# Adaptive modulation as one evenly paced stream of tiles with two buffers of its own, in a two-block network on one Trainium2 core

## The chip, the cores and the metric

The kernel runs on one core of a Trainium2 chip, in float32. The metric is the device time of one execution in microseconds (us): the median of three runs is 2570.3 us (2568.92 to 2570.32).

The engines are TensorE (PE: matrix products, with PEld for the loading of the stationary operand), VectorE (DVE), ScalarE (ACT), GpSimd (POOL) and SyncE (SP), which here issues nearly all transfers. Each engine works through its own instructions in the order in which the program lists them.

## The reference

256 tokens of 1024 features pass a first block of two layers and a second block of two layers. A layer of the first block has three sections: a feed-forward section, a mixer (convolution, state-space and sparse-attention branches, merged by gates), and a second feed-forward section. Ahead of each section the rows are shifted and scaled, and behind it gated, by vectors that depend on a second input `c` alone:

```python
h = x
for l in range(DEPTH):                                   # DEPTH = 2
    mod = (jax.nn.silu(c) @ ada_w[l] + ada_b[l]).reshape(bsz, 3, 3, 1, D_MODEL)
    u = modulate(h, mod[:, 0, 0], mod[:, 0, 1])          # h * (1 + scale) + shift
    y = swiglu_ffn(u, ffn_w_gate[l, 0], ffn_w_up[l, 0], ffn_w_down[l, 0])
    h = layer_norm(DN_ALPHA * h + MACARON_WEIGHT * mod[:, 0, 2] * y, ln_g[l, 0], ln_b[l, 0])
    u = modulate(h, mod[:, 1, 0], mod[:, 1, 1])
    y = hybrid_token_mixer(u, ...)
    h = layer_norm(DN_ALPHA * h + mod[:, 1, 2] * y, ln_g[l, 1], ln_b[l, 1])
    u = modulate(h, mod[:, 2, 0], mod[:, 2, 1])
    y = swiglu_ffn(u, ffn_w_gate[l, 1], ffn_w_up[l, 1], ffn_w_down[l, 1])
    h = layer_norm(DN_ALPHA * h + MACARON_WEIGHT * mod[:, 2, 2] * y, ln_g[l, 2], ln_b[l, 2])
```

`ada_w[l]` has 1024 x 9216 elements: nine vectors of 1024 outputs per layer, 18 in all, here called modulation rows and named (l, j) with j from 0 to 8. Their weights are 75 MB of the 479 MB that the kernel reads. The second block has a mixer and a feed-forward section per layer and no modulation.

## The kernel before

**Weight units.** All weights come in units of 128 x 1024 float32 (512 KB). `load_half` (L177) takes a buffer `raw` from a ring of four (`wraw`, L111) and issues the load on SyncE (L181). `split_half` (L184) then writes the high part `hi` on ScalarE (L187) and the low part `lo` on VectorE (L188) to a second ring of four (`wsp`, L112). TensorE makes three products for each exact one (`hi`x`hi`, `hi`x`lo`, `lo`x`hi`): `gemm_w` (L284 to L286) with the weights stationary, 24 products of 256 columns a unit, or `gemm_x` (L297 to L299) with the activations stationary.

**Order.** The program is written out by hand as a list of items. `run` (L258) walks through it: for each unit it first splits units ahead until four are live (so three units ahead of the one in work), then issues the unit's products and what evacuates them, and last calls `step_sides` (L224). A side is a Python generator with a rate: at each unit it is advanced by that many steps, and each step issues its instructions at that place of every queue. Convolution, attention, state space, early splits of the next section, fetches for the next boundary, and the modulation are sides. `drain` and `force` (L1192) run a side ahead until it is done or a condition holds. `late_load` (L235) places a load behind the last weight load.

**Modulation.** A tile is one eighth of a modulation row: its 128 outputs stand on the partitions, the 1024 weights of each along the columns. `ada_tile` (L493) loads it with `load_half`, so through the same ring of four raw buffers and the same queue as the weights, and one VectorE instruction (L495) multiplies it by the broadcast silu(c) and adds it up into one column. `ada` (L497) is the side that does this for a list of rows, eight tiles a row; after each third row a step turns the row on TensorE (L513) and writes it to DRAM (L516), from where `Ln.fetch` (L572) broadcasts it as the gate of the boundary. silu(c) itself is made by `silu_c` (L479) in a buffer `stk` that the attention uses too; each section that runs tiles loads and transforms it again, by a broadcast load of 512 KB and an activation.

**Who does which rows.** Rows (0,0) and (0,1) are made ahead of the first products (`First.start`). The other 16 are given to sections of the first block by lists at the end (L1881 and after):

```python
nm = 2 if l == 0 else 0
ada0 = [(l, j) for j in range(2 if l == 0 else 3, 8 - nm)]
adam = [(l, j) for j in range(8 - nm, 8)] if nm else []
ada1 = [(l, 8)] + ([(l + 1, j) for j in range(3)] if l + 1 < DEPTH else [])
```

That is 32 tiles in the first feed-forward section, 16 in the first mixer (from its unit 80 on, at 0.75 a unit), 32 in the second feed-forward section, 40 in the third, none in the second mixer, 8 in the fourth feed-forward section. The feed-forward rates (`ffn_section`, L1845) are 0.8, 0.8, 1.0 and 0.6 a unit. `Ln.prefetch` (L563), called ahead of the last units of a section, drains what is left and computes the affine columns of the next section from its shift and scale rows (`mod_affine`, L519).

A later feed-forward section has 11 hidden chunks of four units and 22 units of the down projection, 66 in all; the first makes four of its chunks in `First.start` and has 50 left. A mixer of the first block has 117 units. The convolution's taps (L1187) are 480 VectorE instructions, a side too.

Of the kernel before, what the change touches and what calls it, by code (L numbers as in the profile page):

```python
# [31 lines left out]
# columns of the constant array  # L32
# [16 lines left out]
# columns of the per-layer parameter array of the first block  # L49
# [15 lines left out]
# columns of the per-layer parameter array of the second block  # L65
# [8 lines left out]
class Chunk:  # L74
    """A weight chunk in DRAM, [128, n]; each half loaded when it is split."""
# [19 lines left out]
class Unit:  # L95
    """Half a chunk (1024 columns per partition): split into exact parts, then multiplied by mm."""
# [9 lines left out]
def net_kernel(ctx, tc, a, out, dbg=None):  # L106
# [128 lines left out]
    def late_load(dst, src):  # L235
        # queued behind the weights asked for so far
# [8 lines left out]
    def own_bank(half, key, *ins):  # L245
        # the first half of an accumulator does not wait for the products of the second, in another bank
# [4 lines left out]
    def behind(ins):  # L251
        # what follows is issued after these instructions on their engines
# [26 lines left out]
    def gemm_w(ps, w, xT, wk=0, xk=0, nk=KT):  # L279
        # ps[128 features, 256 tokens]; weights stationary  # L280
# [10 lines left out]
    def gemm_x(ps, xT, k, tt, w, kk, cs, first, last):  # L291
        # ps[128 tokens, n]; activations stationary
# [8 lines left out]
    def tt_split(group, body, between, halves=1):  # L301
        # units held so that all products of token tile 0 come first, then `between`, then token tile 1
# [22 lines left out]
    def proj_cols(src, xT, evac, n=2):  # L325
        # n*128 columns, transposed: evac(ps[128, n*256])
# [10 lines left out]
    def proj_rows(srcs, xT, evac, c=512, between=None, psf=None):  # L337
        # c columns as rows of tokens: evac(tt, ps[128, c]) for both token tiles
# [25 lines left out]
    def row_accum(y, src, xTf, k0, first, last):  # L364
        # y[tt][128 tokens, 1024] += two k-tiles of a chunk
# [14 lines left out]
    def row_tail(y, parts, between, room):  # L380
        # the last k-tiles, token tile 0 first; parts: (chunk, half, operand, k, first)
# [12 lines left out]
    def rows_to_T(row, tt, xT, k0=0, nk=KT, gcol=None, bcol=None):  # L394
        # row [128 tokens, nk*128] -> split transposed operand, with an optional affine per feature
# [22 lines left out]
    def norm_T(norm, row, tt, xT, gcol, bcol=None):  # L418
        # norm(columns) fills part of row; two feature tiles at a time to the split transposed operand
# [38 lines left out]
    def rsqrt_col(dst, src, scale, eps):  # L458
        # dst = (src*scale + eps)^-0.5
# [11 lines left out]
    mods, pcols, adas = {}, {}, []  # L471
# [7 lines left out]
    def silu_c(first=False):  # L479
        crow = f(rt("stk", 8 * P, 1, F32R))  # L480
        if not first:
            late_load(crow, a["c"].to_broadcast([P, D]))
            S.activation(crow, crow, AF.Silu)
            return crow
# [6 lines left out]
        return crow  # L491
# [5 lines left out]
    def ada(items, after=(), crow=None):  # L497
        # silu(c) . w + b, the output features on the partitions
        if crow is None:
            crow = silu_c()  # L500
        for l, j in items:
# [16 lines left out]

    def mod_affine(l, i):  # L519
        # columns G, B with u = n*G + B for the normalised n  # L520
# [22 lines left out]
    def start_fetch(nx):  # L543
        # what the section boundary needs beside the weights, one load per unit
# [1615 lines left out]
```

## Time and profile before

| | before |
|---|---|
| median of 3 runs | 2570.3 us |
| span of the profiled execution, first to last instruction | 2563.5 us |
| TensorE busy | 2443.6 us (95%) |
| VectorE busy | 1847.3 us (72%) |
| ScalarE busy | 1349.5 us (53%) |
| read from memory | 478.79 MB, 189 GB/s over the span |
| modulation tiles in raw buffers | 128 of 512 KB, 156.2 us of VectorE |

The profile is of one execution; its own time outside the span is not given, and the median of the runs lies 6.8 us above the span. Busy time is what an engine spends in instructions; products overlap each other in TensorE's pipeline, so a busy TensorE can still run at less than its full pace, and the count of its instructions in a stretch tells the pace. An idle time ahead of an instruction is put down to the instruction or transfer that ended it. The sections are told apart by their last products, behind which the transposes of the next boundary (L432) follow.

### The profile page before, as it was taken

How to read it: one execution, taken by the hardware profiler on the slowest of the kernel's cores; microseconds unless marked ns; L12 is line 12 of the kernel's file. 1: busy time of each engine (PE TensorE's matmuls, PEld its weight loads, DVE VectorE, ACT ScalarE, POOL GpSimd, SP SyncE). 2: the span in 40 equal slices, each digit the busy share in tenths (PEclk: the TensorE clock that was granted, in tenths of full speed). 3: DMA queues.
4: the chain of work that ended last, by engine and by line, in shares of the span. 5: the costliest groups of instructions: out<-in, count | busy, mean ns of one | idle time of the engine just before them, and what ended most of it. 6: DMA issues, size and time to landing. Idle time of an engine off the chain costs nothing.

```text
span 2563.5 us, 42615 instructions
## 1 busy us (share of the span) xinstructions
PE 2443.6 (95%) x16604; PEld 2205.0 (86%) x16604; DVE 1847.3 (72%) x3270; ACT 1349.5 (53%) x2360; POOL 70.0 (3%) x128
## 2 busy tenths in 40 slices
PE   8988999998999899899999999999899999999999
PEld 6877889898888888788898999899789888789888
DVE  7667888899776677668988996755766545656554
ACT  5334666654553453345666546545465555555554
POOL 0000000000000000000000000000100000100000
PEclk9999999999999999999999999999999999999999
DMA  8886632246868868875522356567345466436464
GB/s 326 271 277 224 197 111 87 80 146 231 290 207 274 291 195 283 269 251 166 164 70 81 123 181 226 195 212 247 123 126 179 159 185 220 139 100 221 141 187 142
DMA packets 134795, 486.83 MB, mean 190 GB/s; under 512 B 15633, under 2 KB 16193, under 8 KB 134594
## 3 DMA queue, kind: packets, MB, share of 16 engines
q1 hardware_dynamic: 134018, 482.93, 57.4%
q8 instruction: 130, 2.13, 0.3%
q10 hardware_dynamic: 576, 1.19, 0.1%
q14 instruction: 71, 0.58, 0.1%
HBM read 478.79 MB, written 5.27 MB: 189 GB/s over the span
## 4 chain that ended last, share of the span: by engine, by line
PE 58%; DMA 17%; DVE 14%; ACT 7%; issue 3%; POOL 1%; ACTq 0%; DVEq 0%; POOLq 0%; SPq 0%
PE mm L284 9%; PE mm L285 9%; PE mm L286 9%; DVE lo L188 6%; PE y L297 6%; PE y L298 6%; PE y L299 6%; DMA raw<-in_wg_dram 4%; DMA raw<-in_adaw_dram 4%; ACT hi L187 4%; DMA raw<-in_wd_dram 3%; DMA raw<-in_wu_dram 3%; DVE ca L1187 3%; PE tp L972 2%; PE tp L963 1%
## 5 line engine op out<-in xcount | busy, mean ns | idle before, releaser
L187 ACT ACTIVATE hi<-raw 128x1024 fp32r<-128x1024 f32 (+1 forms) x676 | 714.2, 1059 | 796.4 <-PE mm L285 285.0
L188 DVE TENSOR_TENSOR lo<-raw,hi 128x1024 fp32r<-128x1024 f32 (+1 forms) x676 | 824.7, 1222 | 385.1 <-ACT hi L187 379.1
L286 PE MATMUL mm<-xTh,lo 128*128 128x256 f32 x2896 | 829.1, 286 | 20.6 <-DVE lo L188 20.5
L284 PE MATMUL mm<-xTh,hi 128*128 128x256 f32 x2896 | 831.9, 287 | 17.5 <-ACT hi L187 9.9
L285 PE MATMUL mm<-xTl,hi 128*128 128x256 f32 x2896 | 825.1, 285 | 1.4 <-DVE xTl L455 1.4
L286 PEld LDWEIGHTS mm<-xTh,lo 128*128 128x128 f32 x2896 | 553.9, 191 | 27.5 <-DVE lo L188 26.9
L284 PEld LDWEIGHTS mm<-xTh,hi 128*128 128x128 f32 x2896 | 554.1, 191 | 26.0 <-ACT hi L187 13.4
L285 PEld LDWEIGHTS mm<-xTl,hi 128*128 128x128 f32 x2896 | 553.6, 191 | 5.2 <-DVE xTl L455 2.2
L299 PE MATMUL y<-hi,q 128*128 128x512 f32 x664 | 263.0, 397 | 0.0
L298 PE MATMUL y<-lo,q 128*128 128x512 f32 x552 | 220.7, 400 | 11.5 <-DVE lo L188 11.4
L297 PE MATMUL y<-hi,q 128*128 128x512 f32 x552 | 220.2, 401 | 4.1 <-ACT hi L187 2.2
L1187 DVE SCALAR_TENSOR_TENSOR ca<-av,pcol,ca 128x244 f32<-128x244 f32 (+22 forms) x480 | 206.8, 460 | 0.5
L495 DVE SCALAR_TENSOR_TENSOR raw<-raw,stk 128x1024 f32<-128x1024 f32 x128 | 156.2, 1221 | 46.6 <-DMA raw<-in_adaw_dram 46.1
L299 PEld LDWEIGHTS y<-hi,q 128*128 128x128 f32 x664 | 125.5, 189 | 30.1 <-DVE q L686 0.4
L298 PEld LDWEIGHTS y<-lo,q 128*128 128x128 f32 x552 | 104.1, 189 | 41.4 <-DVE lo L188 19.8
L297 PEld LDWEIGHTS y<-hi,q 128*128 128x128 f32 x552 | 103.6, 188 | 30.1 <-ACT hi L187 4.4
L297 PE MATMUL y<-hi,xTh 128*128 128x512 f32 (+1 forms) x288 | 113.9, 396 | 2.6 <-DVE e8b L813 1.2
L284 PE MATMUL mm<-xyh,hi 128*128 128x256 f32 x384 | 109.1, 285 | 3.8 <-ACT t2d L1349 3.8
L299 PE MATMUL y<-hi,xTl 128*128 128x512 f32 (+1 forms) x288 | 111.2, 386 | 0.0
L285 PE MATMUL mm<-xyl,hi 128*128 128x256 f32 x384 | 109.3, 285 | 1.7 <-DVE xyl L415 1.7
L298 PE MATMUL y<-lo,xTh 128*128 128x512 f32 (+1 forms) x288 | 110.8, 385 | 0.0
L286 PE MATMUL mm<-xyh,lo 128*128 128x256 f32 x384 | 108.8, 283 | 0.0
(493 smaller groups left out, 3725.0 us busy)
## 6 DMA issues: line engine op xcount, KB each, us to landing
raw<-in_adaw_dram SPq DMA_DIRECT2D x128, 512.0 KB, 5.2
raw<-in_ff_dram SPq DMA_DIRECT2D x128, 512.0 KB, 4.5
raw<-in_wg_dram SPq DMA_DIRECT2D x88, 512.0 KB, 5.3
raw<-in_wu_dram SPq DMA_DIRECT2D x88, 512.0 KB, 5.2
raw<-in_wd_dram SPq DMA_DIRECT2D x88, 512.0 KB, 4.9
raw<-in_wG_dram SPq DMA_DIRECT2D x48, 512.0 KB, 4.8
raw<-in_wkv_dram SPq DMA_DIRECT2D x16, 512.0 KB, 4.8
raw<-in_wval_dram SPq DMA_DIRECT2D x16, 512.0 KB, 5.0
```

What stands on the lines that cost most here:

```text
L187: S.activation(hi, raw, AF.Copy)
L188: eng.tensor_tensor(lo, raw, f(hi), op=ALU.subtract)
L284: E.matmul(ps, wh[:, wk + k], xh, start=(k == 0), stop=False)
L285: E.matmul(ps, wh[:, wk + k], xl, start=False, stop=False)
L286: E.matmul(ps, wl[:, wk + k], xh, start=False, stop=(k == nk - 1))
L297: return [E.matmul(ps, xh, wh[:, kk, cs], start=first, stop=False), E.matmul(ps, xh, wl[:, kk, cs], start=False, stop=False), E.matmul(ps, ...
L298: E.matmul(ps, xh, wl[:, kk, cs], start=False, stop=False),
L299: E.matmul(ps, xl, wh[:, kk, cs], start=False, stop=last)]
L495: V.scalar_tensor_tensor(raw, raw, 1.0, crow, op0=ALU.mult, op1=ALU.mult, accum_out=col[:, k:k + 1])
L963: E.transpose(tp[:, tsl(r * nbr + b)], pr[:, r, b, tsl(kt)], ident)
L972: E.matmul(o[:, i * HD:(i + 1) * HD], pTs[kt][:, tsl(i)], vof(i % nbr, kt), start=(kt == 0), stop=(kt == tt))
L1187: V.scalar_tensor_tensor(ca[:, k, s:T], av[:, 0:T - s], caw[:, k, w:w + 1], ca[:, k, s:T], op0=ALU.mult, op1=ALU.add)
```

## The change

silu(c) is made once, in a buffer `crow` of its own. The tiles of the remaining 16 rows become one generator over the whole first block, `ada_stream`, with a ring `ada` of two buffers; its loads no longer take a `raw` buffer and no longer count as the last weight load for `late_load`. `set_pace` changes its rate at the start of each section so that about 26 tiles fall into each, spread over the section's units. The generator stands at the end of the list of sides. `need` forces it where a boundary wants a row that isn't there. The affine columns are computed in `affine`, called just ahead of the tail of a section, behind the prefetch; it also stops the stream until the next section sets its pace. To make room, the scratch for dynamic DMA descriptors is set to 2048 bytes. The rest of the diff takes comments away.

```diff
-    mods, pcols, adas = {}, {}, []
+    mods, pcols = {}, {}
+    crow = const.tile([P, D], F32, name="crow")
...
-    def ada_tile(l, j, k, crow, col, raw=None):
-        raw = load_half(a["adaw"][l, j, k // 2], k % 2, raw)
+    def ada_tile(l, j, k, col, raw):
+        n = D
+        nc.sync.dma_start(raw, a["adaw"][l, j, k // 2][:, (k % 2) * n:(k % 2 + 1) * n])
         V.scalar_tensor_tensor(raw, raw, 1.0, crow, op0=ALU.mult, op1=ALU.mult, accum_out=col[:, k:k + 1])
...
+    pace = {"after": ()}
...
+    def ada_stream():
+        for l, j in [(l, j) for l in range(DEPTH) for j in range(9)][2:]:
             col = const.tile([P, KT], F32, name="mod%d_%d" % (l, j))
             for k in range(KT):
-                with behind(after):
-                    ada_tile(l, j, k, crow, col)
-                after = ()
+                with behind(pace["after"]):
+                    ada_tile(l, j, k, col, rt("ada", D, 2))
+                pace["after"] = ()
                 yield
...
+    def set_pace(r, after=None):
+        if "gen" not in pace:
+            pace["gen"] = add_side(ada_stream(), 0.0, front=False)
+        for s in sides:
+            if s[0] is pace["gen"]:
+                s[1] = r
+        if after is not None:
+            pace["after"] = after
+
+    def need(*keys):
+        force(pace["gen"], lambda: all(k in mods for k in keys))
...
         def prefetch(self):
-            l, i = self.l, self.i
             drain(state["fetch"])
-            for gen in adas:
-                drain(gen)
             early(self)
-            if not self.last:
-                self.gb = mod_affine(l, i + 1) if i < 2 else mod_affine(l + 1, 0)
+
+        def affine(self):
+            if self.last:
+                return
+            l, i = (self.l, self.i + 1) if self.i < 2 else (self.l + 1, 0)
+            need((l, 3 * i), (l, 3 * i + 1))
+            set_pace(0.0)
+            self.gb = mod_affine(l, i)
...
         def fetch(self):
             l, i = self.l, self.i
-            if i != 1:
-                force(adas[-1], lambda: (l, 3 * i + 2, "row") in mods)
+            need((l, 3 * i + 2, "row"))
...
     def ffn_section(cols, down, nj, act, rows, nxt, tiles):
...
+        us = [i for i, it in enumerate(items) if isinstance(it, Unit)]
+        rate = tiles / (len(us) - 7)
+        if isinstance(src, First):
+            items.insert(us[1], lambda: set_pace(rate, src.ins))
+            items.insert(us[1], lambda: src.finish())
+        elif rate:
+            items.insert(us[3], lambda: set_pace(rate, src.ins))
...
     def mixer_section(fn, l, nxt, tiles=0.0):
...
-            items.insert(units[80], lambda: adas.append(add_side(ada(ada_list, src.ins), 0.75)))
+            rate = tiles / (len(units) - 16)
+            items.insert(units[8], lambda: set_pace(rate, src.ins))
...
-                its, nx = mixer_section(mixer1, l, nxt, adam)
+                its, nx = mixer_section(mixer1, l, nxt, 26.0)
...
-    nc = bacc.Bacc("TRN2", target_bir_lowering=False, num_devices=1)
+    nc = bacc.Bacc("TRN2", target_bir_lowering=False, num_devices=1, dynamic_dma_scratch_size=2048)
```

## Rows read from the trace of the kernel before

**Rows 1.** The page's first section: span, and TensorE's busy time.

```profile
span 2563.5 us, 42615 instructions
PE 2443.6 (95%) x16604; PEld 2205.0 (86%) x16604; DVE 1847.3 (72%) x3270; ACT 1349.5 (53%) x2360; POOL 70.0 (3%) x128
```

**Rows 2.** TensorE's timeline, last product of each first-block section: start us, length us, instruction.

```profile
235.12 0.40 PE L299 MATMUL y<-hi,q 128*128 128x512 f32 x1
...
711.39 0.39 PE L299 MATMUL y<-hi,q 128*128 128x512 f32 x1
...
925.79 0.40 PE L299 MATMUL y<-hi,q 128*128 128x512 f32 x1
...
1150.80 0.40 PE L299 MATMUL y<-hi,q 128*128 128x512 f32 x1
...
1617.02 0.40 PE L299 MATMUL y<-hi,q 128*128 128x512 f32 x1
...
1809.67 0.40 PE L299 MATMUL y<-hi,q 128*128 128x512 f32 x1
```

**Rows 3.** L495 in the third feed-forward section: stretch, its length, VectorE's busy us (records).

```profile
926.10:1151.20 225.10, 49.09 (x80) 0.98 0.76 255
```

**Rows 4.** Short stretches: length, busy us (records) by engine, PE clock, DMA share, GB/s.

```profile
1180.00:1275.00 95.00, 90.12 (x601) 82.13 (x600) 86.17 (x177) 59.11 (x111) 1.63 (x5) 0.98 0.54 175
1280.00:1440.00 160.00, 159.92 (x1199) 142.51 (x1198) 131.33 (x381) 105.46 (x294) 13.83 (x28) 1.00 0.25 78
1450.00:1530.00 80.00, 78.78 (x660) 78.25 (x659) 79.06 (x149) 38.09 (x54) 1.42 (x2) 1.00 0.54 174
...
600.00:650.00 50.00, 41.82 (x337) 40.03 (x336) 45.17 (x75) 25.81 (x42) 1.95 (x2) 1.00 0.80 265
1514.70:1564.70 50.00, 49.33 (x406) 48.11 (x405) 39.07 (x59) 31.34 (x48) 1.10 (x2) 1.00 0.59 189
1675.00:1800.00 125.00, 125.00 (x883) 117.00 (x881) 69.15 (x65) 60.88 (x67) 0.00 (x0) 1.00 0.68 227
```

**Rows 5.** L284, first ordinary unit of the first section: ns min/median/max, first and last start.

```profile
L284 PE MATMUL mm<-xTh,xyh x8: 280/283/364, 66.3 to 69.1; 128*128 128x256 f32 x8
```

**Rows 6.** Waits of SyncE's queue, third feed-forward section: us in total, times, longest.

```profile
SPq L181 <- DVE lo L188: 99.2, 59, 3.1
SPq L181 <- DVE raw L495: 37.5, 36, 3.7
```

**Rows 7.** The page's groups (busy us, mean ns) and a DMA issue (us to landing).

```profile
L187 ACT ACTIVATE hi<-raw 128x1024 fp32r<-128x1024 f32 (+1 forms) x676 | 714.2, 1059 | 796.4 <-PE mm L285 285.0
L188 DVE TENSOR_TENSOR lo<-raw,hi 128x1024 fp32r<-128x1024 f32 (+1 forms) x676 | 824.7, 1222 | 385.1 <-ACT hi L187 379.1
...
raw<-in_wg_dram SPq DMA_DIRECT2D x88, 512.0 KB, 5.3
```

**Rows 8.** Stretches of 25 us of the first, second and fourth feed-forward sections, as rows 4.

```profile
25.00:50.00 25.00, 25.00 (x110) 20.39 (x109) 22.85 (x35) 11.85 (x14) 0.00 (x0) 1.00 0.98 362
...
850.00:875.00 25.00, 20.20 (x124) 17.54 (x123) 16.92 (x22) 11.53 (x13) 0.00 (x0) 0.93 0.83 278
1650.00:1675.00 25.00, 25.00 (x187) 23.83 (x186) 18.01 (x22) 9.61 (x10) 0.00 (x0) 1.00 0.80 269
```

**Rows 9.** VectorE's timeline in the second mixer, one unit of the convolution stretch.

```profile
1459.88 1.22 DVE L188 TENSOR_TENSOR lo<-raw,hi 128x1024 fp32r<-128x1024 f32 x1
1461.01 2.00 DVE L1187 SCALAR_TENSOR_TENSOR ca<-av,pcol,ca 128x250 f32<-128x250 f32 x5
```

**Rows 10.** The chain that ended last: the same taps in both mixers, start and us.

```profile
585.74 4.18 DVE ca L1187 x11
...
1500.37 4.18 DVE ca L1187 x11
```

**Rows 11.** ScalarE's waits from 600 to 650 us, first mixer: us, times, longest.

```profile
ACT hi L187 <- DMA raw<-in_wG_dram: 17.1, 6, 4.9
```

**Rows 12.** L495 over the whole span: VectorE's idle time ahead of it, us and times.

```profile
  DMA raw<-in_adaw_dram: 46.1, 46
```

More of the change, by code (lines that the diff above doesn't have):

```diff
@@ L477, in load_pcol, with silu_c @@
         pcols[l] = t
[L479 to L484, printed above, removed]
+    def silu_c():
         nc.sync.dma_start(crow[0:1], a["c"])
@@ L633, in prefetch, with affine @@
             early(self)
+        def affine(self):
+            pass
         def fetch(self):
@@ L701, in down_items @@
                 ch = Chunk(src[j])
+                items.append([lambda: nxt["nx"].affine()])
                 items.append(row_tail(y, nxt["held"] + [(ch, i, op(j), i, False) for i in range(2)],
@@ L1395, in out_items @@
                     items.append(Unit(ch, kk, D, lambda w, k=k: [row_body(y, op(k), k, tt, w, k == 0, False) for tt in range(2)]))
+        items.append(lambda: nx.affine())
         return items + row_tail(y, parts, lambda: nx.stats(0), lambda: (bt("zc", 4 * T, F32R), bt("vrow", 1040, F32R)[:, :D])), nx
@@ L1786, in modulation @@
                         n += 1
-                        ada_tile(0, j, k, crow, col, room)
+                        ada_tile(0, j, k, col, room)
                 V.scalar_tensor_tensor(sc[:, ks], sc[:, ks], 1.0, adb[:, 0, 8 + 2 * q:10 + 2 * q], op0=ALU.add, op1=ALU.add)
@@ L1843, in net_kernel, with ffn_section @@
     cur = First()
-    def ffn_section(cols, down, nj, act, rows, nxt, ada_list):
+    def ffn_section(cols, down, nj, act, rows, nxt, tiles):
         src = cur
@@ L1848, in ffn_section, with mixer_section @@
         src.pre += set_early(items)
-        if ada_list:
-            def begin():
-                rate = 10.0 * max(len(ada_list), 3) / (6 * nj - 16)
-                adas.append(add_side(ada(ada_list, src.ins, getattr(src, "crow", None)), rate))
-            us = [i for i, it in enumerate(items) if isinstance(it, Unit)]
-            if isinstance(src, First):
-                items.insert(us[1], begin)
-                items.insert(us[1], lambda: src.finish())
-            else:
-                items.insert(us[3], begin)
+        us = [i for i, it in enumerate(items) if isinstance(it, Unit)]
[5 more added lines that the diff above has]
+            items.insert(us[3], lambda: set_pace(rate, src.ins))
         return items, nx
-    def mixer_section(fn, l, nxt, ada_list=()):
+    def mixer_section(fn, l, nxt, tiles=0.0):
         items, nx = fn(l, cur, nxt)
@@ L1880, in net_kernel @@
             prog.append(lambda l=l: load_pcol(l))
-        nm = 2 if l == 0 else 0
-        ada0 = [(l, j) for j in range(2 if l == 0 else 3, 8 - nm)]
-        adam = [(l, j) for j in range(8 - nm, 8)] if nm else []
-        ada1 = [(l, 8)] + ([(l + 1, j) for j in range(3)] if l + 1 < DEPTH else [])
         for i in range(3):
@@ L1938, in prefetch, with affine @@
             self.rows = self.src.rows
+        def affine(self):
+            pass
         def fetch(self):
@@ L1962, in net_kernel @@
             nxt = lambda y, src=cur: Out(y, src)
-        its, nx = ffn_section(lambda j: [a["ff1"][l, j]], a["ff2"][l], DFF2 // T, relu2, lambda ps: relu2(None, ps), nxt, [])
+        its, nx = ffn_section(lambda j: [a["ff1"][l, j]], a["ff2"][l], DFF2 // T, relu2, lambda ps: relu2(None, ps), nxt, 0.0)
         prog += its + close(nx)
```

11 lines of the change are left out of this document (3 added, 8 removed).

## The prediction

> **What bounds the kernel now.** I read the page's first section, then the last product of each section in TensorE's timeline, then the busy time of the engines in short stretches, then the waits of the issuing queue. TensorE is busy for 2443.6 of 2563.5 us [rows 1], so the idle time that could be won is about 120 us, plus stretches in which the products stand less closely than they could. To find them I compare the feed-forward sections, the last three of which run the same products. Their ends [rows 2] give lengths: second 925.8 - 711.4 = 214.4 us, third 1150.8 - 925.8 = 225.0 us, fourth 1809.7 - 1617.0 = 192.7 us. They differ in the modulation tiles: the code gives them 32, 40 and 8 (the third's 80 L495 records, two a tile, agree [rows 3]). The fourth runs at TensorE's own pace, 125.0 of 125 us busy once its tiles are done, and its 66 units take 2.8 us each when some 8 us of boundary are set aside; the convolution stretch of the mixer, where TensorE is busy for 78.8 of 80 us with 660 records, gives 24 x 80/660 = 2.9 us for a unit of 24 products [rows 4]. So I take the fourth section as the floor: the second lies 21.7 us above it, the third 32.3 us.
>
> The first section starts its ordinary units at 66.3 us [rows 5] and ends at 235.1 us [rows 2]. It has 7 x 4 + 22 = 50 units; at 2.8 us they need 140 us, with the transposes about 142 us, so it would end near 208 us. It lies some 27 us above that.
>
> What holds these sections back is the ring of four raw weight buffers. In the third section SyncE stood 99.2 us waiting for the second half of a split (`lo`) and 37.5 us for a modulation product (`raw` L495) before it could issue a load at L181 [rows 6]. A buffer is held for the transfer, 5.3 us, the `hi` copy, 1.06 us, and the `lo` subtraction, 1.22 us [rows 7]: 7.6 us, so four buffers give one load per 1.9 us at best. 106 loads in 225 us are one per 2.1 us: the ring is full. From the second section to the third, 8 tiles more cost 10.6 us, 1.3 us each. The rate of transfer is not the limit by itself: 362 GB/s were moved early on, 278 in a stalled stretch [rows 8].
>
> The mixers of the first block last 476.3 and 466.2 us [rows 2] with 16 tiles and none. VectorE is busy for 86.2 of 95 us in an early stretch, 131.3 of 160 in the attention, 79.1 of 80 while the convolution's taps run beside the first merges, 39.1 of 50 at their end [rows 4].
>
> **The change part by part.**
>
> Tile count. Sixteen of the 18 modulation rows remain, 128 tiles. Every section of the block is paced at 26: per unit 26/43 = 0.60 in the first section, 26/59 = 0.44 in the other feed-forward ones, 26/101 = 0.26 in the mixers (117 units). That makes 27, 27, 26, 26 and 27 steps; after each third row one step carries no tile. The boundaries need 24, 48, 72, 96 and 120 tiles, which are ready at steps 26, 51, 76, 101 and 126; the running sum is 27, 54, 80, 106, 133. So no boundary should force a burst. Tiles go from 32/16/32/40/0/8 to about 26/26/25/25/26/0.
>
> Own buffers. A tile leaves the weight ring. Its load stays on SyncE's queue, behind the weight load of the same unit and ahead of the next. It waits for the product two tiles back, 3 to 8 units ago; the next weight load waits for the subtraction in its slot, four loads back, which VectorE reaches no earlier. So nothing queues up behind the tile's wait. On VectorE the product still stands behind the subtraction of the newest weights and ahead of the next; the tile lands about when those weights do.
>
> Second and third section. Per unit VectorE has 69.2/125 x 2.8 = 1.55 us of work [rows 4] plus 0.44 x 1.23 = 0.54 us (49.09 us for 40 tiles [rows 3]), 2.1 of 2.8. The weights need a buffer every 2.8 us and the ring gives one every 1.9. In the fourth section tiles at 0.6 a unit ran beside a saturated TensorE, 25.0 of 25 us [rows 8]; but that lasted 13 units and could live on what was loaded ahead. Bounds: at 1.3 us a tile the smaller counts alone give 7 x 1.3 = 9 and 15 x 1.3 = 20 us; the whole excess is 22 and 32 us. I take -20 and -30, near the upper end, because the ring's waits are what the rows show.
>
> First section. 76 weight and modulation loads and some 8 others in 142 us are 84 x 0.524 MB / 142 us = 310 GB/s, 86% of the 362 seen [rows 8]; VectorE would have 1.55 + 0.60 x 1.23 = 2.3 of 2.8 us. That is tight, so I take about two thirds of 27 us: -17 (6 x 1.3 = 8 to 25).
>
> Second mixer, 26 tiles from unit 8 on. Early: 21 units, 5.4 tiles, 6.6 us of VectorE, against 8.8 us free in that stretch but in small gaps [rows 4]; about half, +3.5. Attention: 32 units, 8 tiles, 10 us against 28.7 free: +2. Convolution stretch: a `lo` of 1.22 us and five taps of 0.40 us make 3.1 us a unit [rows 9] against 2.8 us of TensorE; 26 units use up some 7 us, about what three units split ahead hold, and TensorE lost only 1.2 us [rows 4]. The tiles add 0.26 x 1.23 = 0.32 us a unit, 8.3 us over 26 units, with no lead left to pay it: +8. Behind it VectorE has room: +1.5. Sum +15, 0.58 us a tile. Ends: 0 (all hidden) and 26 x 1.23 = 32.
>
> First mixer: the same +15, less what its 16 tiles at unit 80 cost now. Up to the convolution's last taps the two mixers run level (350.6 and 349.6 us after their starts [rows 10]), so the difference at the end, 476.3 - 466.2 = 10.1 us, is nearly all theirs, 0.63 us a tile, close to my 0.58. From 600 to 650 us TensorE is busy for 41.8 us against 49.3 in the matching place of the other mixer [rows 4], with ScalarE's `hi` waiting 17.1 us for weights [rows 11]: the ring again. Net +5 (-10 to +22).
>
> The rest has one answer, 0. The fourth section is at its floor. `affine`, now called behind the prefetch, is three operations on 128 x 8 columns ahead of the tail. Of the four broadcasts of `c` that fall away three lie in sections already counted and one in a section at its floor; the six copies of a modulation row to DRAM stay. [...]
>
> Sum: -17 - 20 - 30 + 5 + 15 = -47 us. The span becomes 2563.5 - 47 = 2516.5; the median of the runs lies 6.8 us above the profiled span, so 2523 us.
>
> [...] Where the taps run, VectorE is busy 79.1 of 80 us [rows 4], yet so is TensorE, with 78.8. [...]
>
> **The rivals.**
>
> 1. VectorE is the mixers' bound throughout. Each of 52 tiles costs 1.23 us there: 64 - 10 = +54 against -67 in the feed-forward sections, 2557 us. For it: 79.1 of 80 us. Against: attention and the last merges have room, and 16 tiles cost 0.63 us each. Chance 0.08.
>
> 2. The change doesn't free what it means to free: the order on SyncE or the transfers hold the loads, not the ring. Then only fewer tiles count: -8 - 9 - 20 = -37, with +20 in the mixers -17: 2553 us. For it: a DMA share of 0.83 in a stalled stretch [rows 8]. Against: SyncE's waits for `lo` and `raw` [rows 6]. Chance 0.15.
>
> 3. Slower: in the mixers the product blocks VectorE's queue until its tile has landed, and with it `lo` and every evacuation behind it. Now 46 of 128 waited, 46.1 us [rows 12], 0.36 us on average, so 1.59 us a tile: 52 x 1.59 = 83, less 10, +73 against -67, 2576 us. It decides from 77/52 = 1.48 us a tile. Against: in a mixer the load is issued well ahead of its product, as weights are split three units ahead. Chance 0.05.
>
> 4. The mixers hide their tiles in VectorE's gaps: 0 in one, -10 in the other, so -77: 2493 us. Chance 0.08.
>
> **How the numbers follow.** Forecast 0.64, its own range 2500 to 2545. From 2497 to 2558 I leave out rivals 3 and 4, the upper half of 1 and 2 and the edges of the forecast, 2 in 10. Runs of this kernel can tell about 0.2%, 5 us, from no change. Faster 0.91 (forecast, rivals 1, 2 and 4, less their slow ends), same 0.04 (those ends), slower 0.05 (rival 3).
>
> **What would show it.** The third section lasts some 195 us instead of 225, and SyncE's waits for `raw` L495 are gone; if it stays over 205, rival 2 holds. The second mixer grows to about 481 us, mostly where the taps run beside the merges; 498 would be rival 1. L495 stands evenly from 66 to 1600 us; if VectorE's idle time ahead of it grows past 46 us with `in_adaw` as its end, rival 3 is at work. The forecast is wrong if the mixers together grow by more than 45 us or the feed-forward sections shrink by less than 45.

## The result, and the profile after

The changed kernel takes 2553.36 us (median of 20 runs, 2545.38 to 2566.38) against 2566.91 us (20 runs) for the one before, run beside it: a ratio of 0.9946 with a 95% interval of 0.9934 to 0.9957. It is faster, as forecast, by 0.5%; but the gain is some 14 us where 47 were forecast. The time lies within the 2497 to 2558 us that the prediction gives as its wide range and outside the forecast's own 2500 to 2545.

The page's first section, after:

```profile
span 2552.7 us, 42530 instructions
## 1 busy us (share of the span) xinstructions
PE 2438.5 (96%) x16604; PEld 2208.8 (87%) x16604; DVE 1839.7 (72%) x3270; ACT 1344.2 (53%) x2356; POOL 69.8 (3%) x128
```

TensorE's timeline, last product of each first-block section, as in [rows 2] (start us, length us, instruction):

```profile
220.98 0.40 PE L299 MATMUL y<-hi,q 128*128 128x512 f32 x1
...
719.33 0.39 PE L299 MATMUL y<-hi,q 128*128 128x512 f32 x1
...
932.48 0.39 PE L299 MATMUL y<-hi,q 128*128 128x512 f32 x1
...
1141.80 0.40 PE L299 MATMUL y<-hi,q 128*128 128x512 f32 x1
...
1605.91 0.40 PE L299 MATMUL y<-hi,q 128*128 128x512 f32 x1
...
1799.83 0.40 PE L299 MATMUL y<-hi,q 128*128 128x512 f32 x1
```

The differences of these starts are the sections' lengths. All tables below are made in this way, each from one profiled execution. Sections that carry no tile show how far such lengths scatter: the second mixer of the six kernels without a tile there reads 462.2 to 467.5 us.

| us | before | after | change | forecast |
|---|---|---|---|---|
| first section, to its end | 235.1 | 221.0 | -14.1 | -17 |
| first mixer | 476.3 | 498.4 | +22.1 | +5 |
| second feed-forward section | 214.4 | 213.2 | -1.2 | -20 |
| third feed-forward section | 225.0 | 209.3 | -15.7 | -30 |
| second mixer | 466.2 | 464.1 | -2.1 | +15 |
| fourth feed-forward section | 192.7 | 193.9 | +1.2 | 0 |
| all behind it | 753.8 | 752.8 | -1.0 | 0 |

Where the tiles are: the product (L495 before, L492 after) by section, two records a tile (stretch, its length, VectorE's busy us and records of that line, TensorE's granted clock, DMA share, GB/s), after:

```profile
66.00:221.40 155.40, 32.04 (x53) 0.99 0.84 290
221.40:719.70 498.30, 38.71 (x63) 0.97 0.51 168
719.70:932.90 213.20, 42.82 (x71) 0.98 0.77 258
932.90:1142.20 209.30, 39.88 (x66) 0.97 0.76 254
1142.20:1606.30 464.10, 2.46 (x4) 1.00 0.45 147
```

A product that starts in one section and ends in the next has a record in both, and one more starts at 63.6 us. By their starts that is 27, 32, 35, 32 and 2 tiles, not 26, 26, 25, 25 and 26: the second mixer has hardly any, the second feed-forward section more than it had before (32). And VectorE stands still ahead of the product until a tile lands, 120.5 us in all where it was 46.1 [rows 12]. The idle time ahead of L492 in the whole of after (what ended it, us, times), and then in the third feed-forward section alone:

```profile
  DMA ada<-in_adaw_dram: 120.5, 73
...
  DMA ada<-in_adaw_dram: 43.9, 22
```

Of the 120.5 us, 113.8 lie in the first three feed-forward sections and 6.7 in the first mixer. The end of the second feed-forward section shows what it does. VectorE's timeline there (start us, us, instruction, in brackets the idle time ahead and what ended it):

```profile
908.84 1.22 DVE L188 TENSOR_TENSOR lo<-raw,hi 128x1024 fp32r<-128x1024 f32 x1
913.24 1.23 DVE L492 SCALAR_TENSOR_TENSOR ada<-ada,crow 128x1024 f32<-128x1024 f32 x1 [3.18 <-DMA ada<-in_adaw_dram]
...
914.39 2.36 DVE L188 TENSOR_TENSOR lo<-raw,hi 128x1024 fp32r<-128x1024 f32 x2
916.66 0.68 DVE L808 TENSOR_TENSOR t2d<-t2d,mm 128x512 f32<-128x512 f32 x1
919.71 1.23 DVE L492 SCALAR_TENSOR_TENSOR ada<-ada,crow 128x1024 f32<-128x1024 f32 x1 [2.37 <-DMA ada<-in_adaw_dram]
```

SyncE's timeline, in which the load of the next tile goes out only when the product at 913.24 has freed its buffer, with two weight loads behind it:

```profile
914.50 0.33 SPq L491 DMA_DIRECT2D ada<-in_adaw_dram  x1
915.64 1.47 SPq L181 DMA_DIRECT2D raw<-in_wu_dram  x2
920.98 0.33 SPq L491 DMA_DIRECT2D ada<-in_adaw_dram  x1
```

And TensorE's, which runs out of work when the hidden chunk `q` is late:

```profile
912.88 0.39 PE L299 MATMUL y<-hi,q 128*128 128x512 f32 x1
913.11 0.40 PE L297 MATMUL y<-zc,q 128*128 128x512 f32 x1
918.06 0.79 PE L297 MATMUL y<-hi,q 128*128 128x512 f32 x1 [4.55 <-ACT q L701]
918.65 0.63 PE L298 MATMUL y<-lo,q 128*128 128x512 f32 x1
919.08 0.63 PE L298 MATMUL y<-k,q 128*128 128x512 f32 x1
```

VectorE waits 3.18 us for a tile with two `lo` and the evacuation L808 queued behind it; the tile was asked for too late to be there (its load went out at 907.81 us, and the median landing takes 5.2 us), and nobody needed it yet. TensorE waits 4.55 us for `q` (L701), which ScalarE starts right behind L808, at 917.38 us. Behind the stop a product takes 0.63 us instead of 0.40, and the next one starts 0.43 us later instead of 0.23: from 918 to 927 us the granted clock is 0.50, where it was 1.00 from 905 to 913 us.

The order on VectorE and SyncE is therefore not the order in which the program is written, contrary to what the section on the chip says. The written order is even: a count of `ada_stream`'s steps against the units gives 26, 26, 25, 25 and 26 tiles, where 27, 32, 35, 32 and 2 ran. What put tiles ahead of their written place no row shows; the expectations below call it a planner, which is the author's supposition. Before, a tile's load was held by the weights' ring; now it is held by its own two buffers alone. The first and third experiments test this.

### The profile page after: what moved, and what is told of

The parts are those of the page before. It is cut to its first block, busy times and chain, and to the rows that moved or that the text cites. A ratio compares the mean times of both kernels' runs of the same rounds, so it can differ in the third digit from the quotient of the medians.

```text
span 2552.7 us, 42530 instructions
## 1 busy us (share of the span) xinstructions
PE 2438.5 (96%) x16604; PEld 2208.8 (87%) x16604; DVE 1839.7 (72%) x3270; ACT 1344.2 (53%) x2356; POOL 69.8 (3%) x128
## 4 chain that ended last, share of the span: by engine, by line
PE 61%; DMA 15%; DVE 13%; ACT 5%; issue 4%; POOL 1%; SPq 0%; ACTq 0%; DVEq 0%; POOLq 0%
PE mm L284 10%; PE mm L285 10%; PE mm L286 10%; DMA ada<-in_adaw_dram 8%; PE y L297 6%; PE y L298 6%; PE y L299 6%; DVE lo L188 4%; DVE ca L1204 2%; PE tp L989 2%; ACT hi L187 2%; DMA raw<-in_wg_dram 2%; DVE ada L492 1%; PE tp L980 1%; DMA raw<-in_wo_dram 1%
## 5 line engine op out<-in xcount | busy, mean ns | idle before, releaser
L284 PE MATMUL mm<-xTh,hi 128*128 128x256 f32 x2896 | 827.8, 286 | 10.3 <-ACT av L1222 3.0
L284 PEld LDWEIGHTS mm<-xTh,hi 128*128 128x128 f32 x2896 | 551.2, 190 | 15.9 <-ACT av L1222 3.7
L492 DVE SCALAR_TENSOR_TENSOR ada<-ada,crow 128x1024 f32<-128x1024 f32 x128 | 156.1, 1221 | 120.7 <-DMA ada<-in_adaw_dram 120.5
L1204 DVE SCALAR_TENSOR_TENSOR ca<-av,pcol,ca 128x244 f32<-128x244 f32 (+26 forms) x480 | 207.3, 461 | 0.3
L284 PE MATMUL mm<-xyh,hi 128*128 128x256 f32 x384 | 112.2, 293 | 4.2 <-ACT t2d L1366 4.2
```

The lines of the kernel that those rows point to most:

```text
L284: E.matmul(ps, wh[:, wk + k], xh, start=(k == 0), stop=False)
L1204: V.scalar_tensor_tensor(ca[:, k, s:T], av[:, 0:T - s], caw[:, k, w:w + 1], ca[:, k, s:T], op0=ALU.mult, op1=ALU.add)
```

## The experiments

Each kernel is the changed one with the edit shown. The first theory (A): tiles run ahead of their place, because nothing holds them to the units, and VectorE then waits for them; its rivals are named in each expectation. One table holds the results: medians, the ratio to the kernel before with its 95% interval (none for a kernel run once), the six lengths (the first is the end of the first section), and the tiles by section behind the sixteen at the start.

| kernel | us | ratio | lengths | tiles |
|---|---|---|---|---|
| before | | 1 | 235.1, 476.3, 214.4, 225.0, 466.2, 192.7 | 32/16/32/40/0/8 |
| after | 2553.4 | 0.9946 (0.9934 to 0.9957) | 221.0, 498.4, 213.2, 209.3, 464.1, 193.9 | 27/32/35/32/2/0 |
| e1_pin | 2539.5 | 0.988 (0.9861 to 0.9898) | 209.6, 496.8, 192.4, 199.5, 496.4, 192.9 | 26/26/25/25/26/0 |
| e2_pin3 | 2532.1 | 0.986 (0.9839 to 0.9881) | 209.0, 496.9, 194.0, 198.8, 493.8, 193.3 | 26/26/25/25/26/0 |
| e3_shared | 2615.6 | 1.0184 (1.0165 to 1.0204) | 229.4, 498.7, 218.1, 218.5, 501.0, 195.4 | 26/26/25/25/26/0 |
| e4_none | 2475.0 | 0.9633 (0.9619 to 0.9646) | 209.8, 462.8, 193.6, 194.3, 463.1, 194.3 | none |
| e5_ffn | 2515.4 | 0.9795 (0.9776 to 0.9814) | 228.0, 476.7, 193.3, 196.2, 468.3, 196.4 | 39/10/34/35/3/7 |
| e6_part | 2506.8 | | 208.7, 464.3, 193.1, 197.5, 495.3, 192.5 | 26/26/25/25/26/0 |
| e7_holdload | 2548.2 | 0.9924 (0.9905 to 0.9943) | 212.2, 498.4, 192.6, 197.2, 498.5, 193.0 | 26/26/25/25/26/0 |
| e8_holdprod | 2550.8 | 0.9931 (0.9914 to 0.9948) | 212.6, 498.0, 195.9, 203.3, 491.4, 194.0 | 26/26/25/25/26/0 |
| e9_half | 2554.0 | | 208.4, 481.7, 195.0, 197.2, 521.0, 195.5 | 26/26/25/25/26/0 |
| e10_place | 2536.2 | | 209.8, 496.7, 194.0, 197.8, 482.5, 196.3 | 26/25/25/25/27/0 |
| e11_best2 | 2513.1 | 0.9778 (0.9759 to 0.9797) | 215.6, 486.4, 196.6, 199.5, 464.6, 196.8 | 32/17/38/39/0/2 |
| e12_best3 | 2505.6 | 0.9755 (0.9736 to 0.9774) | 211.0, 489.7, 193.4, 196.2, 467.5, 194.7 | 32/17/38/39/0/2 |
| e13_share | 2497.9 | 0.9713 (0.9696 to 0.9731) | 220.1, 473.0, 195.7, 197.4, 467.0, 193.2 | 40/14/38/36/0/0 |
| e14_free | 2526.1 | 0.9828 (0.9808 to 0.9847) | 218.3, 480.3, 215.8, 200.4, 462.2, 193.9 | 40/24/43/21/0/0 |

**Every tile held to its place.** `behind` puts what follows behind the named instructions on their own engines: the load behind the newest weight load, the product behind the newest `lo`.

```diff
-        eng.tensor_tensor(lo, raw, f(hi), op=ALU.subtract)
+        state["lo"] = eng.tensor_tensor(lo, raw, f(hi), op=ALU.subtract)
...
-                with behind(pace["after"]):
+                with behind(tuple(pace["after"]) + (state["load"], state["lo"])):
                     ada_tile(l, j, k, col, rt("ada", D, 2))
```

> The changed kernel, with every stream tile's load queued on SyncE behind the newest weight load, and its product queued on VectorE behind the newest lo split, so that a tile can't run ahead of its written place. Theory A (the planner of the queues pulls tiles forward because nothing of the unit's pipeline holds them, 35 tiles in the second and third feed-forward sections instead of 25, and VectorE waits behind products whose tile has not landed): 26/26/25/25/26 tiles by section, second feed-forward section 198 to 203 us (213.2 in the changed kernel), third 195 to 200 (209.3), second mixer up to 479 (464.1), in all 2530 to 2545 us, 0.4 to 0.9% under the changed kernel. Theory B (the placement doesn't matter; each tile costs what it costs by its load on VectorE and the transfers): feed-forward sections gain and the second mixer loses the same, within 0.2% of the changed kernel (2553).

Held, the tiles stand 26/26/25/25/26. VectorE's wait for tiles falls from 120.5 us to 3.6, the first of these lines, and in the third feed-forward section SyncE's wait for the product two tiles back from 81.3 us to 5.9; its waits there, after and then held (us, times, longest):

```profile
  DMA ada<-in_adaw_dram: 3.6, 8
```

```profile
SPq L491 <- DVE ada L492: 81.3, 27, 6.5
SPq L181 <- DVE lo L188: 63.3, 58, 4.2
```

```profile
SPq L181 <- DVE lo L188: 118.0, 58, 9.1
...
SPq L491 <- DVE ada L492: 5.9, 8, 1.0
```

The three feed-forward sections shrink by 11.4, 20.8 and 9.8 us against the changed kernel, more in the second than A gave. But the second mixer, with 26 tiles, takes 496.4 us and not 479: there theory B was right. The total came out inside A's range only because the misses offset each other: the sections gained more than A gave, the first one included, for which A had no figure, and the mixer lost 17 us more.

**Three buffers for the stream, held.** `rt("ada", D, 3)` in place of 2.

> As the kernel with every tile held to its written place, with three buffers for the stream in place of two. A: if two buffers still make SyncE wait for the product two tiles back with weight loads queued behind it, 5 to 10 us under the kernel with two; if the hold alone cured it, within 0.2% of that. B: within 0.2%.

The median is 7.3 us lower, the intervals overlap, and the profiled spans are alike (2541.2 and 2540.7 us): so whether the third buffer helps at this share of tiles stays undecided.

**The even spread through the weights' ring.** Not held; the tile's buffer comes from `load_half`, as before.

```diff
-                    ada_tile(l, j, k, col, rt("ada", D, 2))
+                    ada_tile(l, j, k, col, None)
...
-        nc.sync.dma_start(raw, a["adaw"][l, j, k // 2][:, (k % 2) * n:(k % 2 + 1) * n])
+        raw = load_half(a["adaw"][l, j, k // 2], k % 2, raw)
```

> The changed kernel's even spread, but each stream tile takes its buffer from the ring of the weights' raw tiles, as in the kernel before (the two buffers are gone). A (own buffers unpin the tiles): the tile is again held by the ring, 26/26/25/25/26 tiles by section, but VectorE's late products hold the weights' buffers: L495's wait for raw and TensorE's gaps stay; 2545 to 2560 us. B (the spread alone carries the change, own buffers are worth nothing): 2553 within 0.2%. If the own buffers carry it, it goes back to 2565.

The ring does hold the tiles to an even 26/26/25/25/26, but the kernel is slower than before by 47 us, outside all that was expected. SyncE's waits in its third feed-forward section:

```profile
SPq L181 <- DVE lo L188: 74.1, 59, 3.3
SPq L181 <- DVE raw L492: 69.7, 22, 5.9
```

It has the same 25 tiles in that section as the held kernel, and takes 218.5 us against 199.5; the second section 218.1 against 192.4. But the two differ in the tiles' buffers and in the hold at once, and in the whole of this kernel VectorE waits 141.8 us for tiles to land (60 times) against 3.6 in the held one:

```profile
  DMA raw<-in_adaw_dram: 141.8, 60
```

SyncE's 69.7 us for the product show that the ring costs time, as the prediction had it; how much of the 19 to 26 us a section is the ring's and how much the missing hold's is not shown, since no run has held tiles in the shared ring. Spreading by itself only loses: 26 tiles in the second mixer make it 501.0 us.

**No tiles at all** (loads and products of the stream left out).

> The changed kernel without loads and products of the stream's 128 tiles (they are left out; the modulation columns after the first two are set to zero). Gives the floor of each section. A and B: feed-forward sections of the first block near the fourth's 194 us, first section ending near 205, mixers 476 and 464 if the tiles in them are hidden, 440 to 460 if the tiles cost time there; in all 2470 to 2490 us. If the floor is over 2530, the tiles were not what the sections lost by.

The floors are 209.8, 462.8, 193.6, 194.3, 463.1 and 194.3 us. The first mixer comes out 13.5 us below the 476.3 us of before, so there too tiles cost time; the second had none before, and its 466.2 us differ from the floor by no more than that scatter. Against this floor the tiles cost, section by section: before 25, 14, 21, 31, 3 and -2 us; after 11, 36, 20, 15, 1 and 0; held 0, 34, -1, 5, 33 and -1. Held tiles are nearly free in a feed-forward section and cost 1.3 us each in a mixer.

**Loads alone, products alone.** Held; in the first mixer a copy of one column replaces the product, in the second the load is left out and the product takes `crow` twice.

> The kernel with every tile held to its written place, 26 tiles in either mixer, but in the first mixer the tiles are only loaded (their products are left out, a copy of one column reads them), and in the second only multiplied (their loads are left out, the product takes the vector alone). Theory C1 (a mixer pays for the product on VectorE and the TensorE clock that is lost behind it): first mixer 463 to 470, second 490 to 497, against 462.8 and 463.1 without tiles and 496.8 and 496.4 with both. Theory C2 (it pays for the transfers that stand ahead of weights): first 490 to 497, second 463 to 470. Both halves: 475 to 485 each.

Loads alone: 464.3 us, 1.5 over the floor. Products alone: 495.3 us, 32.2 over it. It is the product on VectorE that a mixer pays for, not its tile's landing (3.6 us of waits in the whole held kernel, above). (Each half was tried in one mixer alone; their floors and their prices with both are within 1 us of each other.) The second mixer without tiles, with both (held), and with products alone (busy us of PE, PEld, DVE, ACT, POOL, then clock, DMA share, GB/s):

```profile
1061.00:1524.00 463.00, 451.90 (x3326) 414.55 (x3324) 391.87 (x849) 278.75 (x578) 20.55 (x40) 1.00 0.45 146
```

```profile
1098.60:1595.00 496.40, 470.68 (x3328) 429.60 (x3329) 423.95 (x911) 281.96 (x581) 21.29 (x40) 0.97 0.50 164
```

```profile
1064.00:1559.40 495.40, 467.72 (x3329) 426.19 (x3329) 424.26 (x911) 282.23 (x581) 21.25 (x40) 0.97 0.42 137
```

From the first to the second row VectorE works 32.1 us more and the mixer takes 33.4 us more. Of these TensorE is idle for 14.6 (25.7 against 11.1 us) and busy for 18.8 more with the same products: the granted clock is 0.97 instead of 1.00. Three of its slow stretches in the held kernel (the clock is the third figure from the end):

```profile
1399.40:1406.40 7.00, 7.00 (x35) 7.00 (x35) 5.01 (x12) 1.82 (x4) 0.00 (x0) 0.51 0.44 150
1443.80:1447.20 3.40, 3.40 (x18) 3.40 (x18) 3.40 (x6) 0.00 (x0) 0.00 (x0) 0.51 0.83 280
1474.60:1481.40 6.80, 4.26 (x20) 4.26 (x21) 6.80 (x15) 0.00 (x0) 0.00 (x0) 0.50 0.19 51
```

TensorE's longest waits from 1380 us on in that mixer are for the operands of the merges, which VectorE (L415) and ScalarE (L1266) make:

```profile
PE mm L285 <- DVE xyl L415: 5.0, 1, 5.0
PE mm L284 <- ACT ca L1266: 3.1, 1, 3.1
```

The wait of 5.0 us ends at 1477 us, inside the last of the three stretches. In the ten stretches of 50 us from 1098.2 us on the granted clock is 0.97, 1.00, 0.93, 1.00, 1.00, 1.00, 0.90, 0.93, 0.97 and 0.97: together it falls short by 16.5 us of full clock. TensorE is busy for 473.0 of these 500 us, so by an estimate from these numbers the clock explains some 15 of the 18.8 us. What makes the rest these rows do not show.

**Half a product, and two.** As above, all tiles loaded; half the columns in the first mixer (the rest left out), each product made twice in the second.

> The kernel with every tile held, 26 tiles in either mixer and all of them loaded, but in the first mixer a product takes only half of its tile's columns (the other half is left out) and in the second each product is made twice. Theory E (a mixer pays in proportion to VectorE's time, the product's 1.22 us and the TensorE clock behind it): first mixer 475 to 482 (462.8 without tiles, 496.8 with whole products), second 520 to 535 (463.1 and 496.4). Theory F (it pays once for each extra instruction in the queue, whatever its length): first 490 to 497, second 510 to 530. Theory G (some stretches only, with cover elsewhere): second under 515.

Half a product costs 18.9 us, a whole one 34.0 (33.3 in the second mixer) and two 57.9. VectorE is busy for 17.5, 30.7 (32.1) and 58.4 us more than without tiles; by these sums half a product takes 0.67 us of VectorE (17.5 over 26 tiles), more than half of a whole one's 1.18 (30.7 over 26). So the price goes with VectorE's time (theory E), not with the number of instructions.

**Only the load held, only the product held** (`state["load"]` or `state["lo"]` alone).

> Only the stream tiles' loads are held behind the newest weight load, the products are free in VectorE's queue. If the early issue on SyncE is what shifts the tiles: 26/26/25/25/26 tiles by section and 2535 to 2545 us, as with both held. If VectorE's free product is what hurts: feed-forward sections stay near 205 to 213, 2548 to 2556.

> Only the products are held behind the newest lo split on VectorE, the loads are free on SyncE but have two buffers. If two buffers behind held products are hold enough: 26/26/25/25/26 and 2535 to 2548 us. If loads issued early make weight loads queue behind the product two tiles back, SyncE's waits for that product rise over 150 us in all and it is 2548 to 2560.

Either alone gives the even counts, and neither alone gives the time: their intervals overlap that of the changed kernel. With the load held, the feed-forward sections are within 3 us of their floor; SyncE's wait for the product is 13.4 us in the whole kernel, 230.1 in the changed one. So its first answer came in the counts and the sections, and missed in the time, 2548.2 us. With the product alone held that wait is 168.1 us, as theory two of its expectation said. What either gains in the feed-forward sections the second mixer, with 26 tiles again, gives back.

**Where in a mixer.** Held; the first mixer's tiles in units 8 to 54, the second's from unit 62 on.

> The kernel with every tile held, 26 tiles in either mixer, but in the first all of them in units 8 to 54 (before the convolution stretch), in the second all from unit 62 on (convolution stretch and after). Theory G (the price is in the convolution stretch, where VectorE has the least room): first mixer 472 to 482, second 500 to 515. Theory E (everywhere the same 1.3 us a tile): both 493 to 500.

Theory G falls and stands the other way round: early units pay 33.9 us, the convolution stretch and the merges 19.4 for about as many tiles (0.7 us each), though VectorE is busiest there (79.1 of 80 us [rows 4]). The two places were tried in one mixer each. TensorE's idle time rises from 9.5 to 32.1 us with the early tiles and from 11.1 to 21.9 with the late ones, so most of the early price, 22.6 of 33.9 us, is idle time and not the clock, which is 0.99 there; why the early units are the dearer ones these runs do not show.

**Other shares, held.** The counts per section are changed (table), first for the feed-forward sections to take nearly all:

> The kernel with every tile held to its written place, and the even share given up: 40, 8, 36, 36, 0 and 8 tiles in the six sections of the first block. Theory C (held tiles cost nothing in a feed-forward section, and in a mixer about (496.8 - 462.8) / 26 = 1.3 us each): first section ends at 209 to 214, first mixer 470 to 475, second and third feed-forward sections 193 to 200, second mixer 463, fourth 194; 2490 to 2505 us in all. Theory D (what counts in a feed-forward section is how many tiles it has, 35 being too many, held or not): second and third 205 to 213, 2515 to 2530.

Second and third section stay at 193.3 and 196.2 us with 34 and 35 tiles, which the changed kernel runs in 213.2 and 209.3 with 35 and 32. So it was not the number of tiles there (theory D), it was their order. But the first section ends at 228.0 with 39 tiles, 18 us over its floor, and the total is at D's edge for that reason. The next two put 17 tiles into units 8 to 54 of the first mixer, with two and with three buffers:

> Held tiles, shared out as 33, 17 (all in units 8 to 54 of the first mixer), 40, 40, 0 and 0. By 1.3 us for a mixer's tile and 1.4 us for one over 26 in the first section: 219, 483, 196, 198, 463 and 193 us, with the rest 2503. By theory G (units before the convolution are cheaper) the first mixer is 470 and it is 2490. If 40 tiles are too many for a feed-forward section, 2510 or more.

> The same with three buffers for the stream. If SyncE's waits for the product two tiles back are what a section with 33 to 40 tiles pays, 5 to 12 us under the kernel with two buffers; if not, within 0.2% of it.

40 tiles are not too many for a feed-forward section (193.4 and 196.2 us with 38 and 39). The 17 tiles cost 24 to 27 us in the first mixer, 1.4 to 1.6 each, dearer than any estimate and in line with the run before. The third buffer lowers the median by 7.5 us with intervals that just overlap; the first section ends 4.6 us earlier. So the last share puts the mixer's tiles at unit 80 and later, with three buffers, once held and once not:

```diff
-            rate = tiles / (len(units) - 16)
-            items.insert(units[8], lambda: set_pace(rate, src.ins))
+            items.insert(units[80], lambda: set_pace(tiles / 20.0, src.ins))
...
-                its, nx = mixer_section(mixer1, l, nxt, 26.0)
+                its, nx = mixer_section(mixer1, l, nxt, (8.0, 0.0)[l])
...
-                                      swiglu_rows, nxt, 26.0)
+                                      swiglu_rows, nxt, (41.0, 40.0, 40.0, 0.0)[2 * l + n])
```

> Held tiles, three buffers, shared out as 41, 8 (from unit 80 of the first mixer on), 40, 40, 0 and 0. If the two buffers were what 39 tiles in the first section paid for: that section ends at 211 to 216, first mixer 469 to 475 (0.7 to 0.8 us a tile after the convolution stretch), second and third feed-forward sections 193 to 197, second mixer 463 to 468, fourth 194; 2488 to 2500 us. If 39 tiles are too many for the transfers of the first section: it ends at 224 to 228, 2500 to 2512.

> The same share and buffers, with the tiles not held. If the planner's order is a fault of its own: the tiles run ahead again (over 45 in the second feed-forward section), the feed-forward sections 200 to 215, in all 15 to 30 us over the held one. If the share alone was the fault: within 0.3% of the held one.

Held, this is the fastest version, 2497.9 us, 0.9713 of the kernel before. Its products by section, as above:

```profile
66.00:220.50 154.50, 48.89 (x80) 0.99 0.91 333
220.50:693.50 473.00, 17.11 (x28) 1.00 0.48 161
693.50:889.20 195.70, 46.58 (x76) 1.00 0.83 286
889.20:1086.60 197.40, 44.12 (x72) 1.00 0.80 278
1086.60:1553.70 467.10, 0.00 (x0) 0.99 0.44 145
```

The first section, with 40 tiles, ends at 220.1 us, between the two answers: better than 228.0 with two buffers and 39 tiles, worse than 211.0 with three and 32. That suggests that buffers and count both weigh there. The first mixer got 14 tiles and not 8, at 0.7 us each. Not held, the same share costs 28 us more, tiles run ahead again (43 in the second feed-forward section, not quite the 45 expected, and 21 in the third) and the second section is back at 215.8 us:

```profile
699.10:914.80 215.70, 52.85 (x88) 0.98 0.81 274
914.80:1115.30 200.50, 25.74 (x42) 0.97 0.68 232
```

So both were faults: the share with its third buffer is worth 27 us on the changed kernel (2553.4 to 2526.1), the hold alone 14 (to 2539.5), all together 55, more than the sum of the two.

## Why the prediction was right in sign and wrong in size

The prediction failed at two steps: the step that nothing queues up behind a tile's wait, with the even tile counts that go with it, and the price of a tile in the mixers. By its own last sign the forecast is wrong: the feed-forward sections shrink by 31.0 us, less than 45.

**The floor held; the ring is borne out in part.** Without tiles the second and third sections take 193.6 and 194.3 us, against the 192.7 taken from the fourth [rows 2], and the first ends at 209.8 against my 208. With own buffers and the tiles held, the three sections change by -25.5, -22.0 and -25.5 us against before, -73 in all where -17, -20 and -30 make -67. It is not the smaller counts that gave this: with 38 tiles, held and with three buffers, the second section takes 195.7 us, with 32 before 214.4. So the size of the terms is right; but own buffers without the hold gave -14.1, -1.2 and -15.7, and the ring's own share is not told apart from the hold's. My two thirds for the first section were too careful, my -30 for the third too bold by 4.5.

**The tile counts failed.** I took the written order for the order in the queues, 26/26/25/25/26/0. Nothing but two buffers holds a tile after the change, and 35 and 32 ran in the second and third sections, against 25 and 25 with the hold. The step "nothing queues up behind the tile's wait" failed with it: SyncE stands 81.3 us for the product two tiles back in the third section, and VectorE 43.9 us for landings. It takes about 12 us off the gain in the profiled executions (-22.8 held, -10.8 in the changed kernel), more in the feed-forward sections, less the 32 that the second mixer saves by having 2 tiles instead of 26.

**The mixers' term was mis-sized.** +5 and +15 became +20.5 and +30.2 when the tiles stood where I had put them. My 0.58 us a tile is close to TensorE's added idle time in the second mixer, 14.6 us for 26 tiles, 0.56 each; that may be luck. What the sum left out is that TensorE is busy for 18.8 us more with the same products, some 15 of them (the estimate above) by the granted clock of 0.97: a second term, larger than the first. The bound that I gave, 26 x 1.23 = 32 us, is what was measured (33.3), and I had taken the middle. I had counted VectorE's free time, 8.8 of 95 and 28.7 of 160 us [rows 4], as cover for half and more of the products there; by the proportional price it covered next to nothing.

**The small terms.** Fourth section +1.2 us, all behind it -1.0: the zeros held.

**The rivals.** Of rival 1 (VectorE bounds the mixers) the mechanism is right: held, the mixers grow by 50.7 us against its 54, at a chance of 0.08. Its time of 2557 us lies near the measured 2553 by chance, since the changed kernel has 34 tiles in its mixers and not 52, and its feed-forward sections gain 31 us and not 67. Rival 2's sign came (third section over 205 us, at 209.3), and its 2553 us are the measured time, at a chance of 0.15. Of its two causes the transfers are refuted: held, 38 tiles run through the second section in 195.7 us at 286 GB/s, where the changed kernel takes 213.2 us for 35. The other, the order on SyncE, is what the rows show, in a form that it did not describe: a tile's load that waits for its own buffer, with weight loads behind it. That its time fits is luck in part: its gains came from even counts of 26, 25 and 25 tiles in the feed-forward sections, where 27, 35 and 32 ran, and its +20 us in the mixers came as +22.1 and -2.1, with 34 tiles and not 52. Rival 3's sign came as well, VectorE's wait from 46 to 120.5 us with `in_adaw` as its end, but in the feed-forward sections, where I had not looked for it; in the mixers the products without any load cost the same as with it (495.3 against 496.4 us). Rival 4 is refuted by the same run.

The busy shares alone would not have told what VectorE's time costs in the mixers: it is busy for 391.9 of 463.0 us (85%) in the second mixer without tiles and TensorE's weight loads for 414.6 (90%).

The sum of the miss, in the profiled executions: forecast -47, measured -10.8. The mixers' price, held, takes 31 of the 36 us between (50.7 against 20), the feed-forward terms give 6 back (-73 against -67), and the unheld order takes 12.

## What to carry to other kernels

When work gets buffers of its own, ask what else had held it to its place: the shared ring was a cost and a hold at once, and here most of the gain in the feed-forward sections came only with a new hold, on the load and on the instruction that uses it. Spread filler work by what each section can hide and not evenly, and measure each section's floor by leaving the filler out. Where TensorE has next to no idle time, price every microsecond given to an engine that feeds it at one full microsecond, as the second mixer paid it here (33.4 us for 32.1), unless a run shows cover.

## What the runs showed of the hardware

That one engine's time, spread over a section, is paid in full although it is idle for 15% of it (busy for 391.9 of 463.0 us) was not expected: 32.1 us more of VectorE made a mixer 33.4 us longer, and the doubled product 57.9 us longer for 58.4 more (450.27 against 391.87 busy us). From unit 80 on the price was 0.7 us a tile, so it is not the same everywhere. In the second mixer somewhat less than half of the price, some 15 of 33.4 us by the estimate above, is TensorE's clock, granted 0.97. Without tiles the same mixer is granted 1.00, though TensorE stops there four times for 1.2 to 1.5 us. In the changed kernel's trace, from 60 to 1830 us, stops of 0.7 to 5.3 us, singly (1.2 us and more) or a few close together, are followed or overlapped by thirteen stretches of 3 to 10 us with a granted clock of 0.50; in the one from 918 us on a product of 512 columns takes 0.63 instead of 0.40 us. Five single stops of 1.4 to 1.6 us there have no such stretch behind them. That the clock falls because of the stops is the reading of their places in one trace of each kernel; no run changed the clock alone.

The doubled product's row, from the profile of e9_half:

```profile
1082.70:1603.60 520.90, 477.96 (x3326) 434.02 (x3326) 450.27 (x959) 281.42 (x577) 20.07 (x40) 0.95 0.48 156
```

What stays open: how much of the feed-forward gain is the ring's and how much the hold's, why tiles in a mixer's early units are dearer than those beside the convolution, and how the first section's rest of 10 us divides between buffers, count and transfers (333 GB/s there, 362 the most seen [rows 8]).
